# Attention's weighing in float32 on two halves of the array, with normalisation, weight splits and decayed keys moved

## The chip, the cores and the metric

The kernel runs on one core of a Trainium2 chip. The metric is the device time of one execution in microseconds (us). The core has TensorE (PE: matmuls and transposes into PSUM, fed by weight loads, PEld), VectorE (DVE), ScalarE (ACT), GpSimd (POOL, which works on SBUF only here) and SyncE (SP, which issues most of the DMAs). Each engine takes its own instructions in order, and semaphores order engines among each other.

## The reference

One transformer layer over 512 latent tokens and 256 context tokens, D = 1024, in float32: adaptive norms, one input projection, latent attention (branch A, 8 heads), gated linear attention (branch B, 4 heads), a gated merge, and a gated MLP with a 3x3 depthwise convolution. What the change touches:

```python
# branch A, per head: 512 queries, 768 keys (latent and context), values of 64
s = einsum('bqhd,bkhd->bhqk', qn, k_nope) + einsum('bqhr,bkr->bhqk', qr, k_rope)
p = softmax(s * MLA_SCALE)
o = einsum('bhqk,bkhd->bqhd', p, v)
# branch B, per head and direction, in chunks
decay, u = exp(b_last), einsum('bhncd,bhncv->bhndv', kc * exp(b_last - b_cum), vc)
o = a @ vc + (qc * exp(b_cum)) @ s_in
```

## The kernel before

**Precision.** Most products are made of "split" operands: a high part rounded to `F32R` (`A.copy`, an ACT cast) and the remainder as a low part (`sub`). `mm3` then does three matmuls, high-high, high-low and low-high. A matmul on tiles of type `F32` runs in full float32 without splits.

**Order.** Work is traced in program order, and a planner arranges each engine's instructions by a simulated timeline, except for the engines in `pinned`, which keep program order. During attention PE, V (DVE) and A (ACT) are pinned; G (POOL) is pinned only in short places. Behind attention nothing is pinned, but PE's instructions stay behind the last one of `gla_v`.

**Attention.** `for h in range(NH)` goes over 8 heads, and inside over 6 steps `s`. The half of the queries is `half = s // 3` (256 queries), and `kk = s % 3` is a pair of key blocks (`kt = 2 kk + m`, m = 0 or 1, 128 keys each). A step issues, in this order:

- `turned(h, s + 1)`: four PE transposes of the next step's probabilities into a PSUM tile; ACT casts it to `ph`, DVE subtracts to give `pl`.
- `between(h, s)`: `exped` (ACT: exp of the open scores, with their sum), `scores` of a block of 128 queries of head h + 1 (PE: six matmuls against the keys `kTh`, `kTl`; DVE: the negated maximum `mx`), `normed` (DVE: reciprocal `rs`; POOL: probabilities times `rs`), and at fixed pairs (h, s) the preparation of later heads (`q_mm`, `keys`, `key_parts`), `heads_out` of the head before, and one of eight weight splits for branch B (`gla_v_split(k)`, at the pairs of `gla_steps`, line 921: an ACT cast and a POOL subtraction of 128x512 each).
- `weighed(h, s)`: the product of probabilities and values for this step.

In a head four steps have scores; the last head has matmuls of `gla_v` (branch B's values) in their place.

**The values.** `VV` holds, for each block of 128 keys, 128 columns a head: high and low parts of 64 columns in an order that alternates with the head's parity. So one matmul with the 128 columns as resident operand makes the product with the high part in one half of the PSUM partitions and that with the low part in the other half. `weighed` does four matmuls a step (2 blocks, `ph` and `pl`), each with 256 queries moving, all accumulating in `po`. `heads_out` casts the high half, and adds the other half into the low part `lo` of `oT`.

**Branch B.** `decay(h)` makes the decay factors: `T1`, `T2` for the latent tokens, `C1`, `C2` for the context, `ml` for the chunks. `apply` (line 1136) multiplies them with keys and queries: `Qp` and `T2` for the products inside a chunk, `T1` (keys decayed to the chunk's end) and `Qi` (queries decayed from its start) for the state. `to_tokens` transposes `C1` and `T1` and copies them back (C by DVE, T by ACT). `states` multiplies them with the values, `output` uses `Qp`, `T2` inside chunks (on half-array tiles) and `Qi` with the states `S`. For the first head the order is `decay(0)`, three calls of `gla_v`, `proj_kq(0)`, `apply`, `gate(0)`, `to_tokens`, `states`, `output`.

**Names in the profile.** All engine calls go through one helper, so lines are L87 or L88 (L87: PE behind `gla_v`). `ph`, `pl`, `P`, `mx`, `rs`, `T`, `C`, `S` are the tiles named above; P is shared with `raw` (each head's first two blocks lie in P, the others in raw); `s` is the common pool of 30 buffers (values, queries, oT, Qp, Qi and others), `p` and `pb` are PSUM tiles, `cst` holds the identity matrix of the transposes. `128*64` before a shape means 128 rows and 64 columns of the array.

Of the kernel before, what the change touches and what calls it, by code (L numbers as in the profile page):

```python
# [20 lines left out]
NH = 8  # L21
# [49 lines left out]
def block_kernel(ctx: ExitStack, tc: tile.TileContext, p, out):  # L71
# [25 lines left out]
    def tl(pool, shape, dt, tag, bufs=None):  # L97
        cnt[0] += 1
        kw = {} if bufs is None else {"bufs": bufs}
        return pool.tile(shape, dt, name=f"{tag}_{cnt[0]}", tag=tag, **kw)  # L100
# [14 lines left out]
    def S4(shape, dt=F32R):  # L115
        return tl(s4, shape, dt, "s4")
# [13 lines left out]
    def f(ap):  # L130
        return ap.bitcast(F32)

    def tt(eng, out_, a, b, op):
        return eng.tensor_tensor(out=out_, in0=a, in1=b, op=op)

    def sub(eng, out_, a, b):
        eng.tensor_tensor(out=out_, in0=a, in1=b, op=ALU.subtract)
# [11 lines left out]
    def mm(o, a, b, first=True, last=True):  # L149
        PE.matmul(o, lhsT=a, rhs=b, start=first, stop=last)  # L150
# [7 lines left out]
    def rep(ap, a):  # L158

        return ap.rearrange("p (a b) -> p a b", a=1).broadcast_to([ap.shape[0], a, ap.shape[1]])  # L160
# [174 lines left out]
    with tc.tile_pool(name="e1", bufs=1) as e1:  # L335
# [387 lines left out]
                sub(V, lfs[64 * d + 32:64 * d + 64, 512 * i:512 * i + n], src, f(hi))  # L723


        VV = [S4([128, 1024]) for _ in range(6)]

        kps, turn = [None], [1]

# [44 lines left out]
                mm3(ps, sh, sl, *[w[:, k * 512:(k + 1) * 512] for w in wkv[1]], k == 0, k == 1)  # L774

        def values_out(t, ps):
            v4 = VV[t].rearrange("p (r b d) -> p r b d", r=4, b=4)
            p4 = ps.rearrange("p (r i d) -> p r i d", r=4, i=2)
            A.copy(v4[:, :, 0::3, :], p4)
            sub(V, v4[:, :, 1:3, :], p4, f(v4[:, :, 0::3, :]))  # L780

        q2s, P, open_, exped_ = {}, {h: [] for h in range(NH)}, [], []

        def scores(h, n):

# [18 lines left out]
        def normed(n=4):  # L804

            for pt, rs, sp, mx in exped_[:n]:
                V.reciprocal(rs, rs)
                G.tensor_scalar(out=pt, in0=pt, scalar1=rs, scalar2=1.0, op0=ALU.mult, op1=ALU.mult)
            del exped_[:n]

        def heads_out(h, po):
            i, pr = h % 2, h // 2
            if i == 0:
                oT[pr] = S4([128, 2, 512])
            rw, ro = slice(64 * i, 64 * i + 64), slice(64 - 64 * i, 128 - 64 * i)
            hi, lo = oT[pr][rw, 0, :], oT[pr][rw, 1, :]
            A.copy(hi, po[rw, :])
            sub(V, lo, po[rw, :], f(hi))
            tt(V, lo, po[ro, :], f(lo), ALU.add)

        def turned(h, s):

            half, kk = divmod(s, 3)
            tp = single[s % 2]
            for m in range(2):
                for n in range(2):
                    PE.transpose(tp[:, m * 256 + n * 128:m * 256 + (n + 1) * 128],
                                 P[h][2 * half + n][:, (2 * kk + m) * 128:(2 * kk + m + 1) * 128], ident)
            ph, pl = tl(e1, [128, 512], F32R, "ph", 2), tl(e1, [128, 512], F32R, "pl", 2)
            A.copy(ph, tp)  # L830
            sub(V, pl, tp, f(ph))
            return ph, pl

        def weighed(h, s, po, x2_):

            half, kk = divmod(s, 3)
            vs = slice(h * 128, (h + 1) * 128)
            for m in range(2):
                kt = 2 * kk + m
                for x in x2_:  # L840
                    mm(po[:, half * 256:(half + 1) * 256], VV[kt][:, vs], x[:, m * 256:(m + 1) * 256],
                       kt == 0 and x is x2_[0], kt == 5 and x is x2_[1])


        glav, wv, gps, glv, m0 = [], [], {}, [None], []
# [16 lines left out]
        def gla_v(t, k0=0, k1=KT):  # L862
            if k0 == 0:
                if t % 2 == 0:
                    glav.append(S4([128, 2, 512], F32))
                gps[t] = two[1 - t // 2][:, t % 2 * 512:t % 2 * 512 + 512] if t < 4 else pb()
            for k in range(k0, k1):
                sh, sl = tok(k, t)
                glv[0] = mm3(gps[t], sh, sl, *wv[k], k == 0, k == 7)
            if k1 == KT:  # L870
                A.copy(glav[t // 2][:, t % 2, :], gps[t])

        def between(h, s):

            n = ((0, 1, 2, None, 3, None), (None, 0, 1, 2, 3, None))[h % 2][s]
            even = h % 2 == 0
            if h + 2 < NH and even and s == 5:
                key_parts(1)
            exped()
            if h + 1 < NH and n is not None:  # L880
                scores(h + 1, n)
            if h + 2 < NH and even and s == 5:
                prep_q(h + 2, single[3])
            if h + 2 < NH and not even and s == 1:
                q_parts(h + 2, X_[0])
            if h > 0 and s == (2, 0)[h % 2]:
                heads_out(*pend)
            if h + 2 < NH and not even and s == 0:
                qp = wide()[:, 0:512]
                q_mm(h + 2, qp)  # L890
                X_[0] = q_table(qp)
            normed()
            if h + 2 < NH and (h % 2, s) == (0, 3):
                keys(h // 2 + 1)
                key_parts(0)
            if h == 2:
                next(dw, None)
            if h == 4 and s > 1:
                gla_v_load(s - 2)
            for k in range(KT):  # L900
                if (h, s) == gla_steps[k]:
                    gla_v_split(k)
            if (h, s) == (1, 2):
                pinned.add("G")
                misc_parts()
                pinned.discard("G")
            if h == 0 and s < 2:
                values(4 + s, single[3])
                values_out(4 + s, single[3])
            if (h, s) == (6, 5):  # L910
                begun.append(mp_tile())
                m0.append(mod_steps(3072, begun[0], raw_tile))
                next(m0[0])
                behind["SY"] = load[0]
            if h == 7:
                gla_v(*gla_fill[s])
                for _ in range(2 if s else 0):
                    next(m0[0], None)

        dw, X_ = decay_weights(), [None]  # L920
        gla_steps = [(4, 5), (5, 0), (5, 2), (5, 3), (5, 4), (5, 5), (6, 0), (6, 3)]
        gla_fill = [(0, 0, 2), (0, 2, 4), (0, 4, 6), (0, 6, 8), (1, 0, 4), (1, 4, 8)]

        cb_ = [single[1][:, 0:256], single[1][:, 256:512]]
# [125 lines left out]
            pend = (h, po)  # L1050
        pinned -= {"V", "A"}
        heads_out(*pend)
        gla_v(2)

    def sigmoid(dst, ps):
# [10 lines left out]
    with tc.tile_pool(name="egl", bufs=1) as eg:  # L1066
# [66 lines left out]
        def g8(t_):  # L1133
            return t_.rearrange("p d (a b) -> p (d a) b", a=4)

        def apply(kq, dec):


            gk, gq = kq
            T1, T2, C1, C2, ml = dec  # L1140
            Qp, Qi = S4([128, 2, 512], F32), S4([128, 2, 512], F32)
            tt(G, C1, rep(gk[:, 512:768], 2), C1, ALU.mult)
            tt(V, Qp, rep(gq, 2), T1, ALU.mult)
            tt(V, T2, rep(gk[:, 0:512], 2), T2, ALU.mult)
            tt(V, g8(T1), g8(T2), each(ml[:, 2, :], 128), ALU.mult)
            tt(V, g8(Qi), g8(Qp), each(ml[:, 0, :], 128), ALU.mult)
            return Qp, Qi

        ORDER = ([0, 1, 2, 3], [3, 2, 1, 0])
# [1 line left out]
        def vh(h, t):  # L1151
            return glav[t // 2][:, t % 2, h * 128:(h + 1) * 128]

        def to_tokens(dec):

            T1, T2, C1, C2, ml = dec
            tp, tc_ = p2(), pb()
            for d in range(2):
                for t in range(2):
                    PE.transpose(tc_[:, d * 256 + t * 128:d * 256 + (t + 1) * 128], C1[:, d, t * 128:(t + 1) * 128], ident)  # L1160
            V.tensor_copy(C2, grp(tc_, 2))
            for d in range(2):
                for t in ORDER[d][:3]:
                    PE.transpose(tp[:, d * 512 + t * 128:d * 512 + (t + 1) * 128], T1[:, d, t * 128:(t + 1) * 128], ident)
            A.copy(T1[:, 0, 0:384], tp[:, 0:384])
            A.copy(T1[:, 1, 128:512], tp[:, 640:1024])

        def states(h, dec):
            T1, T2, C1, C2, ml = dec
# [98 lines left out]
        kq = proj_kq(0)  # L1268
        Q = apply(kq, dec)
        gr = gate(0)  # L1270
        to_tokens(dec)
        for h in range(GH):
            St = states(h, dec)
            on = output(h, dec, Q, St)
            if h + 1 < GH:
                dec = decay(h + 1)
                merge_mla(2 * h)
                mod_end()
                kq = proj_kq(h + 1)
            else:  # L1280
                merge_mla(2 * h)
                mod_end()
                mod_begin(S4f)
                merge_mla(2 * h + 1)
            gate_out(h, on, gr)
            if h + 1 < GH:
                Q = apply(kq, dec)
                gr = gate(h + 1)
                to_tokens(dec)
                mod_begin(S4f)  # L1290
                merge_mla(2 * h + 1)

# [293 lines left out]
```

## Time and profile before

| | us |
|---|---|
| median of 3 runs | 902.1 (901.77 to 903.71) |
| the profiled execution | 901.9 |
| its span, first to last instruction | 900.1 |
| attention's steps, first weighing to last, about | 101 to 208 |

Busy shares, stretches and single rows stand in the prediction, where they are used. In a row of the timeline the columns are start, duration (from the first start to the last end where rows of one form are merged), engine, line, operation, out<-in (moving operand first, resident operand second), tile of the array, shape, count, and in brackets the idle time before it and what ended it. In a row of the groups the last columns are busy time, mean ns of one, and idle time before.

### The profile page before, as it was taken

The page shows a single profiled execution, that of the slowest core. Times are in us where ns is not written, and L with a number is a line of the kernel's source. Part 1 is how long each engine was busy: PE and PEld are TensorE (multiplying, and loading weights), DVE is VectorE, ACT ScalarE, POOL GpSimd, SP SyncE. Part 2 cuts the span into 40 slices and gives each one's busy share as a digit, 9 for nine tenths or more (in the row PEclk, how much of TensorE's full clock was granted, in tenths as well). Part 3 has the DMA queues.
Part 4 walks back from the last instruction along what each step waited for, and adds up shares of the span by engine and source line. Part 5 has one row for each costly group of instructions (what it writes and reads, how often), then busy time and mean ns, then how long its engine had stood idle before and what let it go on. Part 6 is the DMA issues. An engine that isn't in the chain of part 4 may idle for free.

```text
span 900.1 us, 12647 instructions
## 1 busy us (share of the span) xinstructions
PE 883.6 (98%) x4870; PEld 749.1 (83%) x4870; DVE 569.1 (63%) x970; ACT 396.2 (44%) x655; POOL 369.1 (41%) x223
## 2 busy tenths in 40 slices
PE   8999999999999999999999999999999999999996
PEld 6888899888888888888887899888888888888885
DVE  4477788776877676745763775987778776300006
ACT  4455676763453545443554233433333333323105
POOL 1612354550624343423653324344444444466404
PEclk9999999999999999999999999999999999999999
DMA  9950001225314242327963313434343432244002
GB/s 315 318 148 1 1 5 33 71 72 164 106 36 129 60 129 59 117 68 253 303 195 92 96 47 119 121 89 141 94 141 104 142 106 94 90 153 151 28 1 94
DMA packets 131436, 100.89 MB, mean 112 GB/s; under 512 B 6826, under 2 KB 121874, under 8 KB 131376
## 3 DMA queue, kind: packets, MB, share of 16 engines
q1 hardware_dynamic: 130256, 97.56, 35.2%
q0 software_dynamic: 864, 2.22, 0.7%
q8 instruction: 38, 0.62, 0.3%
q10 hardware_dynamic: 256, 0.30, 0.1%
q14 instruction: 22, 0.18, 0.1%
HBM read 97.78 MB, written 2.10 MB: 111 GB/s over the span
## 4 chain that ended last, share of the span: by engine, by line
PE 92%; DVE 3%; ACT 2%; issue 1%; POOL 1%; ACTq 0%; DVEq 0%; POOLq 0%
PE pb L88 49%; PE p L88 23%; PE pb L87 14%; PE p L87 6%; DVE s L88 1%; ACT P L88 1%; ACT ph L88 0%; DVE kT L88 0%; DVE mx L88 0%; ACT s L88 0%; DVE P L88 0%; POOL P L88 0%; POOL s L88 0%; POOL wlo L88 0%; ACT kT L88 0%
## 5 line engine op out<-in xcount | busy, mean ns | idle before, releaser
L88 POOL TENSOR_TENSOR wlo<-raw,whi 128x1024 fp32r<-128x1024 f32 (+1 forms) x106 | 239.9, 2271 | 344.4 <-ACT whi L88 312.2
L88 PE MATMUL pb<-s,whi 128*128 128x512 f32 (+1 forms) x906 | 272.1, 383 | 0.0
L88 PEld LDWEIGHTS pb<-s,whi 128*128 128x128 f32 x906 | 167.3, 188 | 32.1
L88 ACT CAST whi<-raw 128x1024 fp32r<-128x1024 f32 (+1 forms) x106 | 103.4, 977 | 177.1 <-issue 72.3
L88 PE MATMUL pb<-s,wlo 128*128 128x512 f32 (+1 forms) x453 | 172.8, 381 | 0.0
L88 DVE SCALAR_TENSOR_TENSOR ac<-pb,cwT,ac 128x441 f32<-128x441 f32 (+2 forms) x160 | 111.0, 694 | 19.2 <-ACT ac L88 15.4
L87 PE MATMUL pb<-s,whi 128*128 128x512 f32 x320 | 101.9, 396 | 0.0
L88 PEld LDWEIGHTS pb<-s,wlo 128*128 128x128 f32 x453 | 85.2, 188 | 16.6
L88 PE MATMUL p<-s,s 128*128 128x512 f32 (+1 forms) x392 | 82.8, 367 | 0.6 <-DVE s L88 0.5
L88 PEld LDWEIGHTS p<-s,s 128*128 128x128 f32 x392 | 65.8, 189 | 14.0 <-issue 2.1
L87 PEld LDWEIGHTS pb<-s,whi 128*128 128x128 f32 x320 | 59.0, 188 | 12.5 <-issue 0.7
L88 PE MATMUL p<-whi,s 128*128 128x512 f32 x208 | 69.0, 392 | 0.1
L88 DVE TENSOR_TENSOR p<-p,gt 128x512 f32<-128x512 f32 x4 | 2.8, 700 | 98.5 <-PE p L88 98.4
L87 PE MATMUL pb<-s,wlo 128*128 128x512 f32 x160 | 62.8, 392 | 0.0
L88 PE MATMUL pb<-whi,s 128*128 128x512 f32 x176 | 57.6, 390 | 0.0
L88 PEld LDWEIGHTS p<-whi,s 128*128 128x128 f32 x208 | 39.0, 188 | 8.4 <-ACT s L88 0.4
L88 DVE TENSOR_TENSOR pl<-pb,ph 128x512 fp32r<-128x512 f32 x48 | 33.0, 687 | 14.8 <-ACT ph L88 14.5
L88 PE MATMUL p<-kT,s 128*128 128x512 f32 (+1 forms) x192 | 41.1, 350 | 1.0 <-ACT P L88 1.0
L88 PE MATMUL pb<-s,s 128*32 128x128 f32 (+2 forms) x322 | 41.2, 315 | 0.6 <-DMA s<-in_w_ada_dram 0.6
L88 ACT ACTIVATE ac<-ac 128x512 f32<-128x512 f32 x22 | 13.9, 633 | 61.4 <-DVE ac L88 61.4
L88 PE MATMUL p<-wlo,s 128*128 128x512 f32 x104 | 40.5, 390 | 0.0
L88 PEld LDWEIGHTS pb<-whi,s 128*128 128x128 f32 x176 | 33.0, 188 | 6.9
(248 smaller groups left out, 1548.1 us busy)
## 6 DMA issues: line engine op xcount, KB each, us to landing
raw<-in_w_up_dram SPq DMA_DIRECT2D x44, 512.0 KB, 3.7
raw<-in_w_in_dram SPq DMA_DIRECT2D x28, 512.0 KB, 3.7
raw<-in_w_down_dram SPq DMA_DIRECT2D x22, 512.0 KB, 3.6
s<-in_w_ada_dram SPq DMA_DIRECT2D x20, 512.0 KB, 5.9
raw<-in_w_ada_dram SPq DMA_DIRECT2D x18, 512.0 KB, 5.0
xn<-in_w_ada_dram SPq DMA_DIRECT2D x10, 512.0 KB, 4.4
kT<-in_w_in_dram SPq DMA_DIRECT2D x8, 320.0 KB, 7.0
s<-in_x_dram SPq DMA_DIRECT2D x4, 512.0 KB, 4.8
```

What stands on the lines that cost most here:

```text
L87: return fn(*args, **kw)
L88: ins = fn(*args, **kw)
```

## The change

1. The values are kept in float32 (`V2`, three buffers in place of six), copied out of PSUM by DVE alone.
2. The transposed probabilities are copied to one float32 tile by ACT; `pl` and its subtraction are gone.
3. `weighed` does two float32 matmuls a step: key block m = 0 into PSUM partitions 0 to 63, m = 1 into 64 to 127, so on the two column halves of the array.
4. `heads_out` adds the two halves on DVE into a float32 tile; two steps later `out_parts` splits it (ACT cast, POOL subtraction).
5. `normed` multiplies on DVE, not on POOL.
6. `gla_steps`: the third to fifth and the later splits move back, so that the sixth head (h = 5) has two in place of five.
7. `apply` makes `T2` and the decayed keys first (now in `Qi`), then `Qp`; the decayed queries are made in `to_tokens`, behind the transposes that read the decayed keys, and overwrite `Qi`.

```diff
-        VV = [S4([128, 1024]) for _ in range(6)]
+        V2 = [S4f() for _ in range(3)]
+        VV = [V2[t // 2][:, t % 2 * 512:t % 2 * 512 + 512] for t in range(6)]
...
         def values_out(t, ps):
-            v4 = VV[t].rearrange("p (r b d) -> p r b d", r=4, b=4)
-            p4 = ps.rearrange("p (r i d) -> p r i d", r=4, i=2)
-            A.copy(v4[:, :, 0::3, :], p4)
-            sub(V, v4[:, :, 1:3, :], p4, f(v4[:, :, 0::3, :]))
+            V.tensor_copy(VV[t], ps)
...
                 V.reciprocal(rs, rs)
-                G.tensor_scalar(out=pt, in0=pt, scalar1=rs, scalar2=1.0, op0=ALU.mult, op1=ALU.mult)
+                V.tensor_scalar(out=pt, in0=pt, scalar1=rs, scalar2=None, op0=ALU.mult)
...
-            hi, lo = oT[pr][rw, 0, :], oT[pr][rw, 1, :]
-            A.copy(hi, po[rw, :])
-            sub(V, lo, po[rw, :], f(hi))
-            tt(V, lo, po[ro, :], f(lo), ALU.add)
+            o_ = EO()[rw, :]
+            V.tensor_copy(o_, po[ro, :])
+            tt(V, o_, po[rw, :], o_, ALU.add)
+            outs.append((oT[pr][rw, 0, :], oT[pr][rw, 1, :], o_))
+
+        def out_parts():
+            hi, lo, o_ = outs.pop()
+            A.copy(hi, o_)
+            sub(G, lo, o_, f(hi))
...
-            ph, pl = tl(e1, [128, 512], F32R, "ph", 2), tl(e1, [128, 512], F32R, "pl", 2)
-            A.copy(ph, tp)
-            sub(V, pl, tp, f(ph))
-            return ph, pl
+            pt = tl(e1, [128, 512], F32, "ph", 2)
+            A.copy(pt, tp)
+            return pt
...
             for m in range(2):
-                kt = 2 * kk + m
-                for x in x2_:
-                    mm(po[:, half * 256:(half + 1) * 256], VV[kt][:, vs], x[:, m * 256:(m + 1) * 256],
-                       kt == 0 and x is x2_[0], kt == 5 and x is x2_[1])
+                mm(po[64 * m:64 * m + 64, half * 256:(half + 1) * 256], VV[2 * kk + m][:, h * 64:h * 64 + 64],
+                   pt[:, m * 256:(m + 1) * 256], kk == 0, kk == 2)
...
+            if outs and s == (4, 2)[h % 2]:
+                out_parts()
...
-        gla_steps = [(4, 5), (5, 0), (5, 2), (5, 3), (5, 4), (5, 5), (6, 0), (6, 3)]
+        gla_steps = [(4, 5), (5, 0), (5, 5), (6, 0), (6, 3), (6, 4), (6, 5), (7, 0)]
...
             tt(G, C1, rep(gk[:, 512:768], 2), C1, ALU.mult)
+            tt(V, T2, rep(gk[:, 0:512], 2), T2, ALU.mult)
+            tt(V, g8(Qi), g8(T2), each(ml[:, 2, :], 128), ALU.mult)
             tt(V, Qp, rep(gq, 2), T1, ALU.mult)
-            tt(V, T2, rep(gk[:, 0:512], 2), T2, ALU.mult)
-            tt(V, g8(T1), g8(T2), each(ml[:, 2, :], 128), ALU.mult)
-            tt(V, g8(Qi), g8(Qp), each(ml[:, 0, :], 128), ALU.mult)
             return Qp, Qi
...
-                    PE.transpose(tp[:, d * 512 + t * 128:d * 512 + (t + 1) * 128], T1[:, d, t * 128:(t + 1) * 128], ident)
+                    PE.transpose(tp[:, d * 512 + t * 128:d * 512 + (t + 1) * 128], Qi[:, d, t * 128:(t + 1) * 128], ident)
             A.copy(T1[:, 0, 0:384], tp[:, 0:384])
             A.copy(T1[:, 1, 128:512], tp[:, 640:1024])
+            tt(V, g8(Qi), g8(Qp), each(ml[:, 0, :], 128), ALU.mult)
```

More of the change, by code (lines that the diff above doesn't have):

```diff
@@ L776, in values_out @@
         def values_out(t, ps):
-            v4 = VV[t].rearrange("p (r b d) -> p r b d", r=4, b=4)
-            p4 = ps.rearrange("p (r i d) -> p r i d", r=4, i=2)
-            A.copy(v4[:, :, 0::3, :], p4)
-            sub(V, v4[:, :, 1:3, :], p4, f(v4[:, :, 0::3, :]))
-        q2s, P, open_, exped_ = {}, {h: [] for h in range(NH)}, [], []
+            V.tensor_copy(VV[t], ps)
+        q2s, P, open_, exped_, outs = {}, {h: [] for h in range(NH)}, [], [], []
         def scores(h, n):
@@ L807, in normed, with EO @@
                 V.reciprocal(rs, rs)
-                G.tensor_scalar(out=pt, in0=pt, scalar1=rs, scalar2=1.0, op0=ALU.mult, op1=ALU.mult)
+                V.tensor_scalar(out=pt, in0=pt, scalar1=rs, scalar2=None, op0=ALU.mult)
             del exped_[:n]
+        def EO():
+            return tl(e1, [128, 512], F32, "pl", 2)
         def heads_out(h, po):
@@ L828, in turned, with weighed @@
                                  P[h][2 * half + n][:, (2 * kk + m) * 128:(2 * kk + m + 1) * 128], ident)
-            ph, pl = tl(e1, [128, 512], F32R, "ph", 2), tl(e1, [128, 512], F32R, "pl", 2)
-            A.copy(ph, tp)
-            sub(V, pl, tp, f(ph))
-            return ph, pl
-        def weighed(h, s, po, x2_):
+            pt = tl(e1, [128, 512], F32, "ph", 2)
+            A.copy(pt, tp)
+            return pt
+        def weighed(h, s, po, pt):
             half, kk = divmod(s, 3)
-            vs = slice(h * 128, (h + 1) * 128)
             for m in range(2):
-                kt = 2 * kk + m
-                for x in x2_:
-                    mm(po[:, half * 256:(half + 1) * 256], VV[kt][:, vs], x[:, m * 256:(m + 1) * 256],
-                       kt == 0 and x is x2_[0], kt == 5 and x is x2_[1])
+                mm(po[64 * m:64 * m + 64, half * 256:(half + 1) * 256], VV[2 * kk + m][:, h * 64:h * 64 + 64],
+                   pt[:, m * 256:(m + 1) * 256], kk == 0, kk == 2)
         glav, wv, gps, glv, m0 = [], [], {}, [None], []
@@ L1052, in block_kernel @@
         heads_out(*pend)
+        out_parts()
         gla_v(2)
@@ L1152, in vh, with to_tokens @@
             return glav[t // 2][:, t % 2, h * 128:(h + 1) * 128]
-        def to_tokens(dec):
+        def to_tokens(dec, Q):
             T1, T2, C1, C2, ml = dec
+            Qp, Qi = Q
             tp, tc_ = p2(), pb()
@@ L1270, in block_kernel @@
         gr = gate(0)
-        to_tokens(dec)
+        to_tokens(dec, Q)
         for h in range(GH):
@@ L1288, in block_kernel @@
                 gr = gate(h + 1)
-                to_tokens(dec)
+                to_tokens(dec, Q)
                 mod_begin(S4f)
```

## The prediction

> **What bounds the kernel now.** I read the busy shares of the page first, then the table of busy time by stretch inside attention, then TensorE's timeline of single steps.
>
> ```profile
> span 900.1 us, 12647 instructions
> PE 883.6 (98%) x4870; PEld 749.1 (83%) x4870; DVE 569.1 (63%) x970; ACT 396.2 (44%) x655; POOL 369.1 (41%) x223
> 141.00:153.00 12.00, 12.00 (x85) 11.09 (x85) 9.99 (x18) 7.82 (x17) 5.27 (x5) 1.00 0.01 1
> 178.00:190.00 12.00, 10.53 (x75) 9.33 (x74) 9.06 (x16) 9.80 (x21) 8.44 (x9) 1.00 0.01 3
> ```
>
> TensorE (PE) is busy 98% of the span. The columns of the last two lines are stretch, length, busy time of PE, weight loads, VectorE (DVE), ScalarE (ACT) and GpSimd (POOL). In the fourth head's steps PE never idles while DVE has 2 us in 12 free; around the sixth and seventh heads PE idles 1.47 us of 12. So a microsecond of DVE or POOL work that goes is worth nothing by itself: only PE time counts, and the few places where PE waits. A busy PE can hide pauses between matmuls, so I measure PE from start to start:
>
> ```profile
> 147.73 0.29 PE L88 MATMUL pb<-ph,s 128*128 128x256 f32 x1
> 147.85 0.28 PE L88 MATMUL pb<-pl,s 128*128 128x256 f32 x1
> 147.97 0.28 PE L88 MATMUL pb<-ph,s 128*128 128x256 f32 x1
> 148.09 0.29 PE L88 MATMUL pb<-pl,s 128*128 128x256 f32 x1
> 148.21 0.60 PE L88 MATMUL pb<-cst,raw 128*128 128x128 f32 x4
> 148.57 1.29 PE L88 MATMUL p<-kT,s 128*128 128x512 f32 x6
> 149.70 0.29 PE L88 MATMUL pb<-ph,s 128*128 128x256 f32 x1
> ```
>
> This is one of the 48 steps (8 heads, 6 steps): four weighing matmuls (`weighed`, moving `ph` or `pl`, resident values), four transposes, six score matmuls. Starts lie 0.12 us apart in the weighing, which takes 0.48 us from 147.73 to 148.21; the step, 1.97 us, is PE end to end. Operands are listed moving first.
>
> **What the new weighing costs on PE.** It removes four full-array matmuls and adds two float32 ones of 64 result columns, one for each half of the array. The trace has float32 matmuls, on the whole array and on halves, in the gated-attention stage:
>
> ```profile
> 298.70 0.60 PE L87 MATMUL p<-s,C 128*128 128x128 f32 x4
> 299.14 0.83 PE L87 MATMUL p<-s,T 128*128 128x128 f32 x6
> 299.81 0.61 PE L87 MATMUL p<-s,C 128*128 128x128 f32 x4
> 300.26 2.32 PE L87 MATMUL p<-s,T 128*128 128x128 f32 x38
> 302.51 0.49 PE L87 MATMUL pb<-S,s 128*128 128x128 f32 x2
> 302.93 0.39 PE L87 MATMUL pb<-s,s 64*128 64x256 f32 x2
> L87 PE MATMUL p<-s,T x176: 219/273/323, 253.6 to 393.4; 128*64 128x128 f32 x64, 128*64 128x64 f32 x64, 128*128 128x128 f32 x48
> L87 PE MATMUL p<-s,C 128*128 128x128 f32 x32 | 4.9, 277 | 1.0 <-ACT T L88 1.0
> L88 PE MATMUL pb<-mp,ones 128*128 128x256 f32 x8 | 2.4, 378 | 0.0
> 15.32 0.28 PE L88 MATMUL pb<-s,wlo 128*128 128x256 f32 x1
> 15.53 0.64 PE L88 MATMUL pb<-s,s 128*32 128x128 f32 x16
> ```
>
> 1. *Two records each.* `states` asks for two C matmuls a direction and the trace has x4: a float32 matmul is two instructions, each 0.44/4 = 0.11 us at 128 moving columns. At 256 columns a record is 378 against 277 ns, 0.10 longer, so 0.21 us.
> 2. *Halves overlap.* The x38 are six full-array ones and, by the form counts over four heads, 16 half-array ones of 128 columns and 16 of 64. From 300.26 to 302.51 is 2.25 us; less 6 x 0.11 that leaves 1.58. One after another the halves would take 16 x 0.11 + 16 x 0.055 = 2.64. Two at a time they take 1.32. So lower and upper half do run together, and 0.26 us is left over.
> 3. *The left-over is entry and exit.* At the entry to a split array alone, 15.32 to 15.53, a 256-column matmul is followed after 0.21 instead of 0.12: **0.09 us of nothing**. The same 0.09 at the exit makes 0.18 of the 0.26; the rest, some 0.05 to 0.08, is the first half-width weight load, which has nothing to hide behind. After the exit the two `S` matmuls take 302.51 to 302.93, 0.42 instead of 0.22: one more entry (0.09) and a full-width first weight load (0.11).
>
> Every step goes from full-array matmuls into halves and back to transposes. A step's weighing then takes 0.09 (entry) + 0.05 (load) + 2 x 0.215 (two pairs of 256 columns) + 0.10 (exit) + 0.05 (first transpose's load: the six transposes at 251.26 below, after a wait, last 0.87, where the four at 148.21 and two more of 0.11 make 0.82) = 0.72 us, against 0.48. That is **+0.24 us, 48 times: +11.5 us**. The streaming alone, 0.43 against 0.48, would have been a small gain.
>
> On entry and exit the Trainium skill, "TensorEngine Tiling (Array Packing)", Key Properties, says that a change of the tiling mode (not of the tile) drains the engine. It gives no price. By that rule all 96 boundaries pay, as in the sum above; without it the sum would be that of the first rival.
>
> Bounds of this term: no entry and exit cost at all gives 0.43 - 0.48, -2.4 us; if accumulating halves do not pair (half A's second instruction ahead of half B's first) a step has three turns of 0.215 instead of two, +21.8 us. I take 11.5, since all the nearest rows are float32 halves of this kernel.
>
> **Waits of PE that should go.** Four stand late in attention, two at its start:
>
> ```profile
> 174.94 0.50 PE L88 MATMUL p<-kT,s 128*128 128x512 f32 x1 [0.29 <-ACT P L88]
> 179.79 0.55 PE L88 MATMUL pb<-cst,P 128*128 128x128 f32 x3 [0.99 <-POOL P L88]
> 185.63 0.50 PE L88 MATMUL p<-kT,s 128*128 128x512 f32 x1 [0.45 <-ACT P L88]
> 190.23 0.38 PE L88 MATMUL pb<-pl,s 128*128 128x256 f32 x1 [0.27 <-DVE pl L88]
> 94.01 0.50 PE L88 MATMUL p<-kT,s 128*128 128x512 f32 x1 [0.22 <-ACT P L88]
> 98.11 0.55 PE L88 MATMUL pb<-cst,P 128*128 128x128 f32 x3 [0.24 <-POOL P L88]
> ```
>
> The first four are 2.00 us idle, and each also loses about 0.16 us of overlap (a record of 0.28 for a start every 0.12): 2.65 us. The longest is a normalisation stuck on POOL behind weight splits; the change moves it to DVE. The last waits for the `pl` subtraction, which goes. The two on `exp` come from splits on ACT between exps; three splits leave the sixth head, and a longer PE step gives ACT more room. I take **-2.65 us**; bounds 0 and -3.4, the latter with the two at the start (0.46 + 0.32), which I leave standing because DVE gets more to do there.
>
> **What DVE, ACT and POOL take on is covered.**
>
> ```profile
> L88 DVE TENSOR_TENSOR pl<-pb,ph 128x512 fp32r<-128x512 f32 x48 | 33.0, 687 | 14.8 <-ACT ph L88 14.5
> L88 DVE TENSOR_REDUCE mx<-p 128x1 f32<-128x768 f32 x32 | 30.3, 948 | 0.2 <-PE p L88 0.2
> L88 DVE RECIPROCAL rs<-rs 128x1 f32<-128x1 f32 x32 | 5.0, 157 | 1.6 <-ACT raw L88 1.3 <-ACT P L88 0.2
> L88 DVE TENSOR_SCALAR s<-s,rr 128x1024 f32<-128x1024 f32 x6 | 5.1, 864 | 0.1
> L88 POOL TENSOR_TENSOR wlo<-s,whi 128x512 fp32r<-128x512 f32 x8 | 10.2, 1285 | 0.0
> ```
>
> A score step on DVE is now 0.69 + 0.95 + 0.16 = 1.80 us. The 0.69 goes; the normalisation comes, 0.864 x 768/1024 = 0.65 us by the x-scaling row, between half of that and the maximum's 0.95. That is 1.4 to 2.1 of a step of 1.97 + 0.24 = 2.21 us. It stands behind the next block's maximum in DVE's program order; what waits for it is the transposes of the next head, mostly a step or more later. If that cover were gone, 32 x 0.65 = 21 us would be exposed; nothing suggests it. The values' eviction becomes one DVE copy in place of an ACT copy plus a 0.69 subtraction; the heads' outputs keep two DVE operations and get an ACT cast and a POOL subtraction two steps later, against a use far behind: nothing. The splits moved to the seventh and eighth head (four in successive steps) cost POOL 1.29 us each per 2.2 us step, ahead of their first use in the last head; no load changes place, so no SP issue moves, and the three buffers that the values give up only make room.
>
> **Decayed keys first.** One wait is left in the gated stage, at its first head:
>
> ```profile
> 251.26 0.87 PE L87 MATMUL p<-cst,T 128*128 128x128 f32 x6
> 253.09 0.68 PE L87 MATMUL p<-s,C 128*128 128x128 f32 x4 [0.95 <-ACT T L88]
> 246.92 3.02 DVE L88 TENSOR_TENSOR s<-gq,T 128x1024 f32<-128x1024 f32 x1 [2.04 <-ACT gq L88]
> 249.98 1.23 DVE L88 TENSOR_TENSOR T<-T,ml 128x1024 f32<-128x1024 f32 x1
> 251.12 1.22 DVE L88 TENSOR_TENSOR s<-s,ml 128x1024 f32<-128x1024 f32 x1
> 252.26 0.69 DVE L88 COPY C<-pb 128x512 f32<-128x512 f32 x1
> 252.23 0.85 ACT L88 COPY T<-p 128x384 f32<-128x384 f32 x2
> ```
>
> DVE's copy of C ends at 252.95 only because the query product (251.12) stands ahead of it. With that product behind the transposes, the copy is done near 252.2 and the C matmuls start; the T matmuls still wait for ACT's first copy, 252.7. I take **-0.8 us**, between 0 and -1.1. The other three heads show no such wait, so they gain nothing; the query product has until the `S` matmuls, which in the next head come 3.8 us behind the first C matmul (298.70 and 302.51).
>
> **Sum.** 901.9 us (this profiled execution: span 900.1 and 1.8 around it) + 11.5 - 2.65 - 0.8 = 909.95. The three timed runs have a median of 902.1, 0.2 above: **910 us, slower by 0.9%.**
>
> **Rivals.**
> *Faster: the entry and exit are waits, not switches.* The first instruction after each boundary also carries a dependence; if 0.09 is what a met dependence costs there, it is already inside the old steps and disappears. Place: the 96 boundaries. With x for entry, exit and loads of a step, the change costs 48 (x - 0.05) - 3.45, so it wins below x = 0.12; I read 0.29. At x = 0: 901.9 - 2.4 - 3.45 = 896 us. Against it: `weighed` also waits for ACT and DVE each step and keeps its 0.12. By the Trainium skill's drain rule it falls, and the trace agrees with 0.09 at 15.53. Chance 0.09.
> *Halves do not pair when they accumulate.* The paired rows are single products, these are sums over three. 901.9 + 21.8 - 3.45 = 920 us. Chance 0.07.
> *The waits stay* (four splits in a row in head seven, DVE's normalisation late): 901.9 + 11.5 = 913.4 us. Chance 0.17.
> *Entry and exit are half hidden* by the queue ahead: x about 0.12, no change, near 902. Chance 0.05.
> The forecast holds the remaining 0.62, from 906 to 912.
>
> **The numbers.** A difference under 0.2% (1.8 us) can't be told from none here. Faster 0.10, same 0.06, slower 0.84, from the cases above with a little for surprises. The range reaches from 904 (more waits gone, trips of 0.15) to 917 (trips of 0.32, waits kept); it leaves out the first, the second and part of the fourth case.
>
> **What would show it.** In the new timeline the first half-array matmul of a step should start about 0.21 us after the last score matmul, the pair's second 0.27 later, the first transpose 0.31 after that; a score step should last 2.2 us. The `P` and `pl` waits of PE should be gone between 174 and 200, attention should end some 9 us later, and everything behind should only be shifted. A step of 1.9 us proves the forecast wrong on the switch; one of 2.4 on the pairing; a DVE that idles nowhere in attention, on the cover.

## The result, and the profile after

The changed kernel takes a median of 910.22 us (4 runs, 910.18 to 911.77) against 901.98 for the kernel before: a ratio of 1.0091, 95% interval 1.0079 to 1.0104. It is **slower by 0.9%**, 8.2 us; forecast were 910 us.

The page's head, of the changed kernel:

```profile
span 908.4 us, 12545 instructions
PE 894.8 (99%) x4870; PEld 734.5 (81%) x4870; DVE 570.1 (63%) x954; ACT 390.7 (43%) x649; POOL 349.6 (38%) x199
```

TensorE has as many instructions as before and is busy 11 us more, at a higher share. VectorE has changed its work, not its load (569.1 before). The step that the prediction took apart, in TensorE's timeline of the changed kernel:

```profile
151.56 1.30 PE L88 MATMUL p<-kT,s 128*128 128x512 f32 x6
152.79 0.65 PE L88 MATMUL pb<-ph,s 128*64 128x256 f32 x4
153.37 0.66 PE L88 MATMUL pb<-cst,raw 128*128 128x128 f32 x4
153.78 1.29 PE L88 MATMUL p<-kT,s 128*128 128x512 f32 x6
155.01 0.65 PE L88 MATMUL pb<-ph,s 128*64 128x256 f32 x4
```

A step now lasts 2.22 us (152.79 to 155.01), where it lasted 1.97. The weighing is one row of four instructions on 64 columns; from its start to the first transpose are 0.58 us (before: 0.48 for four full-array matmuls), although by the prediction's count the values stream no longer than before (0.43 us against 0.48). The transposes take 0.41 us to the first score matmul, 0.36 before, and the pause ahead of the weighing, 0.09 us, is the rest. In the single records behind these merged rows the first pair starts 0.21 us after the last score matmul, the second pair 0.27 later and the first transpose 0.31 after that: the three distances that the prediction gave as its signs.

The table of stretches, attention of the kernel before (first line) and of the changed one; columns as in the prediction:

```profile
97.00:213.00 116.00, 113.78 (x729) 101.54 (x728) 86.14 (x147) 74.42 (x141) 54.43 (x56) 1.00 0.21 63
97.00:222.00 125.00, 124.47 (x729) 86.45 (x728) 82.22 (x132) 72.51 (x138) 38.09 (x33) 1.00 0.19 58
```

TensorE idled 2.2 us in the old stretch and 0.5 in the new: most of the waits went, and the stretch still grew by 9 us with the same 729 instructions. GpSimd has 16 us less to do in it and VectorE 4 us less, and it is longer all the same.

Some executions of a kernel, of the one before too, lose 1.3 to 2 us ahead of attention, so profiled executions are compared by stages and kernels by their medians. Measured from start to start, over the whole kernel:

| us | before | after | difference |
|---|---|---|---|
| up to the first transpose of probabilities | 97.61 | 97.52 | -0.1 |
| from there to the first decay matmul (48 steps) | 115.78 | 124.78 | **+9.0** |
| of it waits of TensorE | 4.10 | 0.97 | -3.13 |
| of it all else | 111.68 | 123.81 | **+12.13** |
| from there to the first C matmul (gated stage, first head) | 39.71 | 39.14 | -0.6 |
| from there to the last matmul | 638.67 | 638.63 | 0.0 |

A wait is counted here as the time from start to start beyond what the same matmuls take elsewhere without it, from 0.06 us on, so it is more than the idle time of the rows. The 0.97 us that are left stand at the start of attention, where TensorE waits for the first normalisations. The first head's wait in the gated stage, TensorE and then VectorE of the changed kernel:

```profile
260.40 0.82 PE L87 MATMUL p<-cst,s 128*128 128x128 f32 x6
261.44 0.68 PE L87 MATMUL p<-s,C 128*128 128x128 f32 x4 [0.22 <-DVE C L88]
260.61 0.69 DVE L88 COPY C<-pb 128x512 f32<-128x512 f32 x1 [1.46 <-PE pb L87]
261.26 3.30 DVE L88 TENSOR_TENSOR s<-s,ml 128x1024 f32<-128x1024 f32 x1
```

The copy of C now stands ahead of the query product and starts when the transposes allow it; of 0.95 us idle 0.22 are left. In both kernels the T matmuls follow 0.52 us behind the first C matmul, so the wait for ScalarE's first copy, which the prediction left standing, is not there.

### The profile page after: what moved, and what is told of

The parts are those of the page before. It is cut to its first block, busy times and chain, and to the rows that moved or that the text cites. A ratio compares the mean times of both kernels' runs of the same rounds, so it can differ in the third digit from the quotient of the medians.

```text
span 908.4 us, 12545 instructions
## 1 busy us (share of the span) xinstructions
PE 894.8 (99%) x4870; PEld 734.5 (81%) x4870; DVE 570.1 (63%) x954; ACT 390.7 (43%) x649; POOL 349.6 (38%) x199
## 3 DMA queue, kind: packets, MB, share of 16 engines
q0 software_dynamic: 864, 2.22, 0.8%
## 4 chain that ended last, share of the span: by engine, by line
PE 94%; DVE 2%; ACT 1%; DMA 1%; issue 0%; SPq 0%; DVEq 0%; ACTq 0%
PE pb L88 51%; PE p L88 24%; PE pb L87 14%; PE p L87 6%; DMA raw<-in_w_ada_dram 1%; DVE s L88 1%; DVE P L88 0%; DVE kT L88 0%; ACT P L88 0%; ACT s L88 0%; DVE mx L88 0%; SPq L88 0%; ACT kT L88 0%; DVE X L88 0%; ACT rr L88 0%
## 5 line engine op out<-in xcount | busy, mean ns | idle before, releaser
L88 ACT COPY ph<-pb 128x512 f32<-128x512 f32 x48 | 28.2, 587 | 36.0 <-PE pb L88 36.0
L88 DVE TENSOR_REDUCE mx<-p 128x1 f32<-128x768 f32 x32 | 30.4, 954 | 17.2 <-PE p L88 17.0
```

Of the source, the lines that this page charges most:

```text
L88: ins = fn(*args, **kw)
```

## The experiments

In the tables of this section "stage" is the time from the first transpose of probabilities to the first decay matmul, as above.

### Fewer trips into halves

The changed kernel with the weighing of 2, 3 or 6 steps done together; only the loop and the place of the transposed probabilities differ:

```diff
+            if s % 2 == 0:
+                pts[0] = S4f()
-            pt = tl(e1, [128, 512], F32, "ph", 2)
+            pt = pts[0][:, s % 2 * 512:s % 2 * 512 + 512]
...
-                weighed(h, s, po, step)
+                held.append((h, s, po, step))
+                if s % n == n - 1:        # n = 2, 3, 6
+                    for w_ in held:
+                        weighed(*w_)
+                    held.clear()
```

> The changed kernel, but the weighing of two steps is done together, so TensorE goes into halves 24 times instead of 48; matmuls, transposes, copies and dependences are the same. Theory (each entry into halves and exit from them costs a fixed time on TensorE, 0.29 us a trip with the first weight loads): 24 x 0.29 = 7.0 us less, 910.2 - 7.0 = 903.2 us. Rival (the pause belongs to the dependence of each first matmul on ScalarE's copy, which every step keeps): 910 us.

> As before, but the weighing of three steps together: 16 trips. Theory: 32 x 0.29 = 9.3 us less, 900.9 us. Rival: 910 us. If 900.9 holds, it is within 0.2% of the kernel before.

> As before, but all six steps of a head together: 8 trips. Theory: 40 x 0.29 = 11.6 us less, 898.6 us, faster than the kernel before (902.0) by about 3.4 us, which is the waits that the change took away. Rival 1: 910 us. Rival 2: the sum of a head now comes late for the head's output and VectorE, in order, stands still there: above 900 us.

| | trips | median us (ratio, interval) | stage | of it waits | stage without waits |
|---|---|---|---|---|---|
| changed kernel | 48 | 910.2 | 124.78 | 0.97 | 123.81 |
| e1_pairs | 24 | 907.1 (1.0060, 1.0045 to 1.0075) | 121.86 | 5.00 | 116.86 |
| e2_threes | 16 | 903.8 (1.0022, 1.0013 to 1.0032) | 118.54 | 4.05 | 114.49 |
| e2_sixes | 8 | 909.8 (1.0085, 1.0067 to 1.0104) | 124.62 | 12.47 | 112.15 |

The ratios are to the kernel before. Without waits the stage falls by 6.95 us for 24 trips, by 9.32 for 32 and by 11.66 for 40: **0.29 us a trip**, all three times. The weighing still waits for ScalarE's copies as before, so the pause belongs to the switch, and the rival of the dependence falls. The medians miss what I expected (903.2, 900.9, 898.6), because I had left out new waits. In e1_pairs the steps alternate:

```profile
151.04 1.08 PE L88 MATMUL pb<-s,s 128*64 128x256 f32 x8
152.06 0.66 PE L88 MATMUL pb<-cst,raw 128*128 128x128 f32 x4
152.47 1.30 PE L88 MATMUL p<-kT,s 128*128 128x512 f32 x6
153.60 0.60 PE L88 MATMUL pb<-cst,raw 128*128 128x128 f32 x4
154.28 1.31 PE L88 MATMUL p<-kT,s 128*128 128x512 f32 x6
```

Two steps take 4.48 us (151.04 to 155.52), of which 0.32 are a wait: the four transposes at 153.60, with no switch ahead of them, should hand over after 0.36 but take 0.68, held up by an exp. The 4.16 that are left are 0.28 less than two steps of 2.22: the price of one trip, within rounding. A pair of weighings takes 1.02 us (151.04 to 152.06) where two single ones take 1.16. Steps without weighing are short, and ScalarE and VectorE don't keep up. With six together it is plain; TensorE's timeline of e2_sixes, its total from the list of waits, and a row of VectorE's timeline:

```profile
196.79 0.84 PE L88 MATMUL pb<-cst,P 128*128 128x128 f32 x3 [2.29 <-DVE P L88]
PE pb L88 <- DVE P L88: 5.1, 5, 2.3
195.12 1.61 DVE L88 TENSOR_SCALAR P<-P,rs 128x768 f32<-128x768 f32 x1
```

The next head's probabilities are not normalised when the sixth step wants to transpose them; four such waits, and the one at the start of attention that the changed kernel has too, idle TensorE for 5.1 us. Shortly ahead of each of the four stands a normalisation of 1.6 to 1.7 us (last row) instead of 0.62, beside a subtraction on GpSimd; the last section comes back to this. Rival 2 expected a late sum for the head's output; the wait stands at the normalisation instead.

### Both blocks in one half

```diff
-                mm(po[64 * m:64 * m + 64, half * 256:(half + 1) * 256], VV[2 * kk + m][:, h * 64:h * 64 + 64],
-                   pt[:, m * 256:(m + 1) * 256], kk == 0, kk == 2)
+                mm(po[0:64, half * 256:(half + 1) * 256], VV[2 * kk + m][:, h * 64:h * 64 + 64],
+                   pt[:, m * 256:(m + 1) * 256], kk == 0 and m == 0, kk == 2 and m == 1)
```

> The changed kernel with both key blocks sent to the lower half of the array one after the other (the addition of the two halves is left out on VectorE, as there is one sum only). Trips stay 48. Theory (the two halves run together in the changed kernel): two turns of 0.215 us become four, 48 x 0.43 = 20.6 us more, 930.8 us. Rival (accumulating halves do not overlap, and the pause is smaller than read): 910 to 915 us.

Measured in one run: 930.5 us, 20.3 over the changed kernel, 0.42 a step. TensorE of e3_one_half:

```profile
152.26 1.08 PE L88 MATMUL pb<-ph,s 128*64 128x256 f32 x4
153.27 0.66 PE L88 MATMUL pb<-cst,P 128*128 128x128 f32 x4
```

The same four instructions take 1.01 us to the first transpose where they take 0.58 in two halves. So accumulating products of the two halves do run together, and the second rival of the prediction falls.

### Trips that depend on nothing

The kernel before, with a pair of float32 matmuls on constants in the middle of 38 products of the MLP (additional work, read by nobody):

```diff
+                if spare and k == 3:
+                    for m in range(2):
+                        mm(spare[0][64 * m:64 * m + 64, 0:128], ident[:, 0:64], ident)
```

> The kernel before with 38 added trips into halves in the upward projection of the MLP, where TensorE never waits: in the middle of each product of the last 19 blocks one pair of float32 matmuls (identity by identity, 128 moving columns, one for each half) into a PSUM tile that nobody reads. Their operands are constants from the start, so they depend on nothing. Theory (a switch costs its time by itself): entry 0.09 + load 0.05 + two turns of 0.11 + exit 0.10 + full-width load 0.11 = 0.57 us, 38 times 21.7, 923.5 us. Rival (the pause is the dependence of the first matmul): two turns of 0.11 alone, 38 x 0.22 = 8.4, 910.2 us.

Measured in one run: 924.6 us, 22.8 over the kernel before, 0.60 a trip. TensorE of e7_free_trips:

```profile
602.52 0.39 PE L88 MATMUL pb<-s,wlo 128*128 128x512 f32 x1
602.84 0.44 PE L88 MATMUL p<-cst 128*64 128x128 f32 x4
603.21 0.73 PE L88 MATMUL pb<-s,whi 128*128 128x512 f32 x2
603.78 0.39 PE L88 MATMUL pb<-s,wlo 128*128 128x512 f32 x1
```

A 512-column matmul, after which the next starts 0.23 us later in this kernel, is followed by the half-array pair after 0.32: 0.09 us of entry, with operands that have been there since the start. The pair, two turns of 0.11, hands over after 0.37, and the two full-array ones behind it take 0.57 instead of 0.46, which fits a first weight load with nothing to hide behind. Together that is 0.09 + 0.37 + 0.11 = 0.57 us, as expected, and the same in all 38 places; some 0.02 more are spread over the matmuls behind.

### Parts of the change on the kernel before

Three kernels: the decayed keys alone; these and the moved splits; the normalisation on VectorE alone (the diffs are those of the change, points 7, 6 and 5).

> The kernel before with only the decayed keys first. Theory (one wait of TensorE at the first head of the gated stage gets shorter, nothing else): 901.8 - 0.65 = 901.2 us, not told from none in the times but from the trace: the first C matmul comes 39.1 us after the first decay matmul, before 39.7. Rival (the planner gives it back elsewhere): 901.8 us or more.

> The kernel before with only the moved splits and the decayed keys first; weighing, values, outputs and normalisation as before. Theory (the halves cost 11.6 us on TensorE, and the rest of the change is what removes waits): 901.8 - 2.65 (the four late waits of attention) - 0.65 (the wait in front of the first states) = 898.5 us. Rival (those waits went only because the longer step gave ScalarE and GpSimd room): they come back in the seventh head, where four splits now follow each other, and the time is 900 to 902 us.

> The kernel before with only the normalisation moved from GpSimd to VectorE. Theory (VectorE's step becomes 0.69 + 0.95 + 0.16 + 0.65 = 2.45 us against TensorE's 1.97, so this part needs the other): VectorE becomes the bound in the steps with scores, 903 to 908 us. Rival (the normalisation on GpSimd was what TensorE waited for, and VectorE has the room): 900.7 us.

- e5_keys: 900.99 against 901.75, ratio 0.9993 (0.9983 to 1.0002), not told from none by the times. In the trace the first C matmul comes 38.86 us after the first decay matmul, 0.85 earlier than before, and everything behind it keeps its 638.7.
- e4_steps_keys: 900.09 against 901.75, ratio 0.9984 (0.9974 to 0.9993). **It beats both kernels**, the one before by 0.16%. I expected 898.5: of the four late waits only that on GpSimd's normalisation went. TensorE of e4_steps_keys:

```profile
175.27 0.50 PE L88 MATMUL p<-kT,s 128*128 128x512 f32 x1 [0.29 <-ACT P L88]
184.76 0.73 PE L88 MATMUL p<-kT,s 128*128 128x512 f32 x2 [0.43 <-ACT P L88]
189.35 0.38 PE L88 MATMUL pb<-pl,s 128*128 128x256 f32 x1 [0.27 <-DVE pl L88]
```

They have the size of before (0.29, 0.45, 0.27), though the casts around them have moved.

- e6_norm: 910.4 us in one run, above the 903 to 908 expected; stage 123.12, 7.3 longer than before. VectorE's busy time in the stage is 106.87 of 123.20 (86.14 of 116.00 before), and the longest waits of TensorE's weight loads in this stage of e6_norm lead to it, three directly and one through ScalarE's exp, which itself waits for VectorE's maximum:

```profile
PEld p L88 <- ACT P L88: 3.2, 5, 1.1
PEld pb L88 <- DVE pl L88: 3.0, 6, 1.4
PEld pb L88 <- DVE P L88: 2.1, 3, 0.9
PEld pb L88 <- DVE s L88: 1.6, 3, 0.8
```

So here the normalisation on VectorE costs 7.3 us as long as the `pl` subtraction stays there. The rival, 900.7, falls.

### Where the splits matter

```diff
-        gla_steps = [(4, 5), (5, 0), (5, 5), (6, 0), (6, 3), (6, 4), (6, 5), (7, 0)]
+        gla_steps = [(4, 5), (5, 0), (5, 5), (6, 5), (7, 0), (7, 1), (7, 1), (7, 2)]   # e8, on e4_steps_keys
+        gla_steps = [(4, 5), (5, 0), (5, 2), (5, 3), (5, 4), (5, 5), (6, 0), (6, 3)]   # e9, on the changed kernel
```

> The kernel before with the decayed keys first and with the splits still later than in the change: the last five in the steps from the end of the seventh head on, where the eighth head has no exps. Theory (of the three late waits that are left in e4_steps_keys, those at the third and fifth step of the seventh head, 0.60 + 0.43 us, come from ScalarE's casts just ahead of them): 900.1 - 1.0 = 899.1 us. Rival (they come from ScalarE's exp and VectorE's subtraction themselves, or the last splits now come too late for the matmuls that need them): 900 us or more.

> The changed kernel with the splits at their old steps. Theory (in the changed kernel the four late waits went because the step became longer and the normalisation left GpSimd, not because the splits moved): no wait of TensorE between 100 and 220 us, 910.2 us. Rival (the moved splits are needed there too): the waits on exp come back, 911 to 912 us.

e8_late_splits: 900.85 against 901.97, ratio 0.9991 (0.9982 to 1.0000), no better than e4_steps_keys: its stage is 115.64 us long against 114.59, by short new waits in the last head, where the late splits are needed. The same three waits stand in the trace with the same sizes: the casts don't cause them, and the theory falls. e9_old_steps: 910.8 us in one run, between theory and rival. Of the four waits one is there, now on VectorE; TensorE and VectorE of e9_old_steps:

```profile
187.19 0.55 PE L88 MATMUL pb<-cst,P 128*128 128x128 f32 x3 [0.38 <-DVE P L88]
182.62 2.92 DVE L88 TENSOR_SCALAR P<-P,rs 128x768 f32<-128x768 f32 x1
```

It is the one at which the prediction's longest stood (179.79), 0.38 us idle instead of 0.99. The normalisation ahead of it lasts 2.92 us, beside a subtraction and a weight split that follow each other on GpSimd; without the split it lasts 1.68 in the changed kernel. So the moved splits remove this wait in both kernels, and the other three go with the rest of the change, whatever the splits do: the longer step and the leaner VectorE are the likely reasons, which no run separates. What starts these three in the old step was not tried further.

## Why the prediction was right, and where its reasons were not

- **Entry, load and exit (+11.5 us).** Right, and so is the mechanism: 12.13 us measured from start to start, 0.25 a step against the 0.24 of the sum. A pure trip is 0.29 us (e1, e2), as the prediction read it, and the streaming saves some 0.04 of the 0.05 it assumed. e7 shows the price where nothing can be waited for. With the rule of the Trainium skill, "TensorEngine Tiling (Array Packing)", Key Properties, that a change of the tiling mode drains TensorE, the traces agree: 0.09 us pass at the entry (e7, 602.52 to 602.84), and in the changed kernel the first transpose starts 0.31 us after the second pair, 0.09 more than the 0.22 of a pair.
- **Halves overlap.** Right: e3 loses 0.42 us a step without it, against the 0.43 worked out.
- **Waits of TensorE (-2.65 us).** Near in size (-3.13), the reasons half right. From start to start the four late waits were 3.0 us, short ones of 0.6 us in all went too, and one at the start of attention grew by 0.5. The longest did stand on a normalisation behind weight splits, but it is not the move to VectorE that removes it: with the splits at their old steps TensorE still waits for it there (e9), and with the splits moved the wait goes on GpSimd too (e4). For the two on exp the prediction named splits between the exps, and e8 shows them unchanged with the splits elsewhere. Its second reason, the longer step, is left, as one part of the rest of the change. The wait for the `pl` subtraction went with the subtraction.
- **Start of attention.** The two waits there stay, as forecast, but the sum had nothing for the second one's growth: 0.23 and 0.47 us idle after, 0.22 and 0.24 before.
- **Cover on VectorE.** Right in sum, and its step had room. The size of the normalisation, 0.65, hides two values: it is 0.62 in most cases and up to 1.69 us in some.
- **Decayed keys (-0.8 us).** Alone they give 0.85 (e5), in the changed kernel 0.6: there a low split that GpSimd finishes late holds TensorE at 240.6, and two matmuls follow after 0.37 and 0.34 us instead of 0.23 each.
- **Rivals.** Faster through free switches: refuted by e1, e2 and e7. Half hidden: refuted by the same 0.29. No pairing: refuted by e3. The waits stay: most went.
- **Slips in its sums.** The rival in which the waits stay, 913.4, leaves out the decayed keys; with them it is 912.6. The outer ends of the range do not come out of their conditions: by the prediction's own formula trips of 0.15 with its waits gone give 903.3 us, not 904, and trips of 0.32 with the waits kept 914.9, not 917. Neither touches the forecast.

## What to carry to other kernels

Splitting TensorE's array pays only if much is streamed per entry: a trip cost 0.29 us in these attention steps whether it carried one weighing or six, so work on halves belongs together, and where it alternates with full-array work every step pays twice. Where TensorE is the bound, taking work from VectorE and GpSimd is worth their few waits and no more: here 3.1 us, for 12.1. And work gathered into rarer, longer pieces must leave the other engines' rhythm alone: six weighings at once saved 11.7 us of TensorE and lost 11.5 to new waits.

## What had not been expected of the hardware

VectorE's normalisation of 128x768 takes 0.62 us, but up to 1.69 in the changed kernel when GpSimd runs a two-input subtraction beside it. The two rows (minimum, median, maximum in ns) of that kernel, its GpSimd beside the query product at 261.26 shown above, and GpSimd of the kernel before beside the same product at 251.12:

```profile
L88 DVE TENSOR_SCALAR P<-P,rs x16: 620/622/1691, 94.1 to 196.5; 128x768 f32<-128x768 f32 x16
L88 DVE TENSOR_SCALAR raw<-raw,rs x16: 619/621/1616, 99.8 to 201.1; 128x768 f32<-128x768 f32 x16
261.11 2.37 POOL L88 TENSOR_TENSOR wlo<-raw,whi 128x1024 fp32r<-128x1024 f32 x1 [3.05 <-ACT whi L88]
251.92 2.64 POOL L88 TENSOR_TENSOR wlo<-raw,whi 128x1024 fp32r<-128x1024 f32 x1 [3.05 <-ACT whi L88]
```

Five of the 32 last longer than 1.1 us, three of them beside the subtraction of `out_parts`, which the change itself put on GpSimd. The query product takes 3.30 us at 261.26; in the kernel before, at 251.12, it took 1.22, although GpSimd's split began beside it 0.80 us later. Which of the two begins first matters: in the seven kernels that normalise on VectorE, 224 normalisations in all, those over 0.8 us lie beside work of GpSimd that began before them or at most 0.04 us after, and where GpSimd's subtraction alone begins 0.09 us or more behind, the normalisation keeps 0.62. The sign stood in the prediction's own rows: the product at 246.92 lasts 3.02 us, beside a split that GpSimd began at 246.47, and in the changed kernel the second head's takes 1.21 at 296.41, with GpSimd idle.

The Trainium skill, "GPSIMD Engine Reference", Specifications, says that GpSimd shares its SBUF interfaces with VectorE's instructions that have two SBUF inputs or run in a two-port mode. The query product, with two inputs, agrees; that the normalisation, with one such input, is of the second kind, no run shows. The rows add that the instruction on VectorE may last nearly as long as both together (3.30 us, where 1.22 and 2.37 make 3.59).
